# Block-product gates: high weights against paired high and low tokens in one 512-column matmul, weight sums by accumulating transfers

## The chip, the cores and the metric

The kernel runs on one core of one Trainium2 chip. The metric is the device time of one execution in microseconds (us). Three runs of the kernel before took 1444.5, 1445.52 and 1447.1 us, a median of 1445.52 us.

On the core, TensorE (PE) multiplies, VectorE (DVE) and ScalarE (ACT) work on tiles in SBUF and read TensorE's results from PSUM, GpSimd (POOL) does almost nothing in the kernel before, and SyncE (SP) issues every transfer. Each engine executes its own instructions in order and waits on semaphores for the others.

## The reference, cut to what matters

One layer of a hybrid decoder trunk for 512 tokens of 2048 features. From a normalised input `h` come nine projections; two branches (a causal convolution and a differential attention) are gated, projected and merged by sigmoid gates, and projected once more:

```
h = rms_norm(x, g_pre) * (1 + scale) + shift          # shift, scale, gate = split(silu(c) @ w_ada + b_ada)
cv, cg, cz, q, k, v, az, m_conv, m_attn = split(h @ w_in)
y_conv = (silu(layer_norm(conv(cv * sigmoid(cg)))) * silu(cz)) @ w_conv_out
y_attn = (rms_norm(diff_attention(q, k, v)) * (1 - lam0) * silu(az)) @ w_attn_out
out    = (sigmoid(m_conv) * y_conv + sigmoid(m_attn) * y_attn) @ w_o
x      = x + gate * rms_norm(out, g_post)
```

The change concerns three of the projections of `h`: `cz` (1024 columns of `w_in`), `m_attn` and `m_conv` (2048 columns each), called cz, ma and mc in the kernel.

## The kernel before, in words

Features lie on the partitions, tokens along the free axis. Every fp32 operand of a matmul is the sum of two float32r parts, high and low: ACT casts the high part (`split`, L141), DVE subtracts it to get the low part (L142). A product is then three matmuls into one PSUM bank (`mm3`, L163): high by high, high by low, low by high; low by low is left out.

In time the stages are: normalised input and convolution gates (to about 258 us), values, queries, keys and attention (to about 620 us), the az gate with the sums of token blocks (to 679 us), **the gates cz, ma, mc** (679.5 to 1086 us), the projections of the two branches (to 1260 us) and the output projection.

The gates stage is 20 blocks of 256 output columns: four of cz, eight of ma, eight of mc. One block (`gemm_blocks`, L649) cuts `h` into 2x2 blocks (halves of the features by halves of the tokens) and the weights likewise into a11, a12, a21, a22, and computes the result by seven products of block sums instead of eight. The token sums T1 to T4 were made in the stage before (`block_sums`). The weight sums s1 = a21 + a22, s2 = s1 + a11, s3 = a11 + a21 and s4 = s2 + a12 are made in each block by four DVE additions over 128x1024 (L673, L674, L683, L692).

One product multiplies eight 128x128 weight tiles by eight 128x256 token blocks: 8 x 3 matmuls of 256 columns. The seven products use three banks: z (twice), x (three times: T2, T3, T4) and y (twice). In order of time they are z with B11, x with T2, y with T1, x with T3, z with B21, x with T4, y with B22. A later product of a bank adds to what the bank holds, so what DVE needs of the earlier state is read between the two: after x with T2, `u2 = q1 - x` (L679) must have read x before x with T3 may write. q1 is ACT's copy of z (L676). L682, L686, L691 and L695 are the other combinations, one DVE read of 128x256 each.

The raw weights come in two transfers of 1 MB (`wraw`, tiles `wr`, three buffers). The split weights use three buffers each for high (`wh`) and low (`wl`): the split for a product needs the buffer of the product three before it, so it waits for that product to end.

In the ma blocks DVE and ACT also finish the attention output of one head pair, `o * az` (L788), and split it (`oh`, `ol`); o and az are fetched from DRAM by SP, in SP's order behind the spills of the block before.

The matmuls of the stage keep the program's order (a token, `ordered`). The order on DVE and ACT is written out by the Tile framework's scheduler when the kernel is built; nothing in the program fixes it.

Of the kernel before, what the change touches and what calls it, by code (L numbers as in the profile page):

```python
# [51 lines left out]
def hybrid_trunk(ctx: ExitStack, tc: tile.TileContext, x, c, w_ada, b_ada, g_pre, g_post, w_in,  # L52
# [526 lines left out]
    T23, T4 = [None] * KH, [None] * KH  # L579
    t1s = [temp(f"t1_{i}") for i in range(KH // 2)]  # L580

    def block_sums():
        for _ in range(SKIP):
            yield
        for k in range(KH):
# [18 lines left out]
            if k % 2:
                hi, lo = page(f"t4h_{k}", F32R), page(f"t4l_{k}", F32R)
                split(t4, hi, lo, pace=True)
                for i in range(2):
                    T4[k - 1 + i] = (hi[:, i * H2:(i + 1) * H2], lo[:, i * H2:(i + 1) * H2])
                yield
# [17 lines left out]
    B11 = [(hi[:, :H2], lo[:, :H2]) for hi, lo in h[:KH]]  # L627
    T1 = [(hi[:, H2:], lo[:, H2:]) for hi, lo in h[:KH]]
    T2 = [(hi[:, :H2], lo[:, :H2]) for hi, lo in T23]
    T3 = [(hi[:, H2:], lo[:, H2:]) for hi, lo in T23]  # L630
    B21 = [(hi[:, :H2], lo[:, :H2]) for hi, lo in h[KH:]]
    B22 = [(hi[:, H2:], lo[:, H2:]) for hi, lo in h[KH:]]
# [16 lines left out]
    def gemm_blocks(src, c0, name):  # L649
        """Two output tiles [128 features, tokens] of h @ src[:, c0:c0+256], by 7 products of 2x2 blocks.  # L650

        a11 a12 / a21 a22: features by halves of the sum.  Returns (c11 in PSUM, [.. c12], [c21 c22])."""
# [42 lines left out]
        nc.vector.tensor_tensor(u2, u2, y[:, :H2], op=ALU.add)  # L695
        return z, ta, tb

    def silu2(i, z, ta, tb):
# [2 lines left out]
        nc.scalar.activation(g0[:, :H2], z[:, :H2], AF.Tanh, scale=0.5)
        nc.scalar.activation(g0[:, H2:], ta[:, H2:], AF.Tanh, scale=0.5)
        nc.scalar.activation(g1, tb, AF.Tanh, scale=0.5)
        nc.vector.scalar_tensor_tensor(g0[:, :H2], g0[:, :H2], 1.0, z[:, :H2], op0=ALU.add, op1=ALU.mult)
        nc.vector.scalar_tensor_tensor(g0[:, H2:], g0[:, H2:], 1.0, ta[:, H2:], op0=ALU.add, op1=ALU.mult)
        nc.vector.scalar_tensor_tensor(g1, g1, 1.0, tb, op0=ALU.add, op1=ALU.mult)
# [271 lines left out]
```

## Time and profile before

| | us |
|---|---|
| median of 3 runs (lowest, highest) | 1445.52 (1444.5, 1447.1) |
| span of the profiled execution | 1448.4 |
| gates stage in it (first z_cz matmul to first py_ya matmul) | 679.5 to 1085.9 |
| TensorE busy | 1413.6 (98%) |
| VectorE busy | 1053.0 (73%) |
| ScalarE busy | 534.2 (37%) |
| GpSimd busy | 1.8 |

The span runs from the first to the last instruction of the profiled execution; it was 2.9 us longer than the median of the timed runs, so what lies around the span doesn't show as extra time here, and the two differ by less than the spread of the runs (2.6 us) plus 0.3 us. "Busy" counts the engines' own work, not the issuing of transfers. Matmuls overlap in the pipeline, so the mean time of one matmul in the groups (283 ns for 256 columns) is longer than the distance from one matmul to the next; that distance is the length of a run of matmuls in the chain of waits over their count.

### The profile page before, as it was taken

The numbers are of one execution on the slowest core, as the hardware profiler recorded it, in microseconds if no ns is written. First come the engines' busy times: TensorE is split into PE (matmuls) and PEld (weight loads), VectorE is DVE, ScalarE is ACT, GpSimd is POOL, SyncE is SP. The second block draws the span as 40 slices with busy tenths as digits, with TensorE's granted clock in tenths as the row PEclk, the third lists the DMA queues.
The fourth block names the chain that finished last, engine by engine and source line by source line (L and its number), as shares of the span: only waits on it lengthen the run. The fifth ranks groups of instructions, "written<-read, shape, count | busy, mean of one in ns | idle before, by whom it ended". The sixth has DMA issues, their size and how long they took to land.

```text
span 1448.4 us, 20732 instructions
## 1 busy us (share of the span) xinstructions
PE 1413.6 (98%) x8191; PEld 1200.4 (83%) x8191; DVE 1053.0 (73%) x1720; ACT 534.2 (37%) x901; POOL 1.8 (0%) x8
## 2 busy tenths in 40 slices
PE   4999999999999999999999999999999999999997
PEld 4776778787777877688999999999998888888885
DVE  4466785988888888588997888877767448656645
ACT  4622233223444244434544444444445323222230
POOL 0000000000000000000000000000000000000000
PEclk9999999999999999999999999999999999999999
DMA  9878653232223323124654555533369647267543
GB/s 285 264 255 291 215 167 130 88 131 87 66 81 102 102 67 109 66 95 135 209 165 160 187 178 191 188 121 132 126 226 349 224 137 233 95 207 243 189 145 145
DMA packets 178466, 238.62 MB, mean 165 GB/s; under 512 B 7793, under 2 KB 118722, under 8 KB 177474
## 3 DMA queue, kind: packets, MB, share of 16 engines
q1 hardware_dynamic: 178370, 237.31, 49.5%
q8 instruction: 64, 1.05, 0.3%
q14 instruction: 32, 0.26, 0.1%
HBM read 210.02 MB, written 27.26 MB: 164 GB/s over the span
## 4 chain that ended last, share of the span: by engine, by line
PE 93%; DVE 3%; DMA 1%; ACT 1%; issue 1%; SPq 0%; DVEq 0%; ACTq 0%
PE pc L163 12%; PE pw L163 12%; PE py_ya L163 6%; PE py_yc L163 6%; PE pv L163 6%; PE pg_k L163 6%; PE pg_q L163 5%; PE pg_az L163 5%; PE x_ma L163 5%; PE x_mc L163 5%; PE y_mc L163 3%; PE z_mc L163 3%; PE z_ma L163 3%; PE y_ma L163 3%; PE x_cz L163 2%; PE y_cz L163 2%
## 5 line engine op out<-in xcount | busy, mean ns | idle before, releaser
L468 DVE SCALAR_TENSOR_TENSOR cacc<-u,cw,cacc 128x511 f32<-128x511 f32 (+14 forms) x240 | 164.4, 729 | 0.0
L163 PE MATMUL pc<-hh,wh_c 128*128 128x512 f32 x256 | 102.9, 408 | 1.1 <-ACT hh L141 1.1
L163 PE MATMUL pc<-hh,wl_c 128*128 128x512 f32 x256 | 101.0, 398 | 1.5 <-DVE wl_c L142 1.4
L163 PE MATMUL pc<-hl,wh_c 128*128 128x512 f32 x256 | 101.7, 397 | 0.0
L339 DVE TENSOR_TENSOR part<-pc,part 128x512 f32<-128x512 f32 x96 | 66.0, 691 | 46.9 <-PE pc L163 45.8
L163 PE MATMUL pw<-wh_o,mh 128*128 128x512 f32 x224 | 89.0, 397 | 0.0
L163 PE MATMUL pw<-wh_o,ml 128*128 128x512 f32 x224 | 87.3, 390 | 0.0
L163 PE MATMUL pw<-wl_o,mh 128*128 128x512 f32 x224 | 87.2, 389 | 0.0
L141 ACT CAST wh_c<-wr_c 128x1024 fp32r<-128x1024 f32 (+1 forms) x36 | 34.6, 960 | 112.5 <-PE pc L163 85.6
L141 ACT CAST wh_o<-wr_o 128x1024 fp32r<-128x1024 f32 x28 | 29.5, 1053 | 104.5 <-PE pw L163 93.0
L163 PEld LDWEIGHTS pc<-hh,wh_c 128*128 128x128 f32 x256 | 49.0, 192 | 17.9 <-issue 3.3
L856 DVE SCALAR_TENSOR_TENSOR accg<-adag,cact,accg 128x512 f32<-128x512 f32 x60 | 45.0, 750 | 24.0 <-DMA adag<-in_w_ada_dram 22.8
L163 PEld LDWEIGHTS pc<-hh,wl_c 128*128 128x128 f32 x256 | 49.1, 192 | 15.7 <-issue 2.5
L142 DVE TENSOR_TENSOR wl_o<-wr_o,wh_o 128x1024 fp32r<-128x1024 f32 x28 | 34.2, 1221 | 34.0 <-ACT wh_o L141 34.0
L163 PEld LDWEIGHTS pc<-hl,wh_c 128*128 128x128 f32 x256 | 49.3, 192 | 10.2 <-issue 0.4
L163 PE MATMUL pv<-wh_v,hh 128*128 128x512 f32 x128 | 51.2, 400 | 0.9 <-DVE part L339 0.9
L142 DVE TENSOR_TENSOR wl_c<-wr_c,wh_c 128x1024 fp32r<-128x1024 f32 (+1 forms) x36 | 39.7, 1104 | 16.5 <-ACT wh_c L141 16.4
L163 PE MATMUL pg_q<-hh,wh_q 128*128 128x512 f32 x128 | 51.1, 399 | 0.0
L163 PE MATMUL pg_k<-hh,wl_k 128*128 128x512 f32 x128 | 51.1, 399 | 0.0
L163 PE MATMUL pg_q<-hl,wh_q 128*128 128x512 f32 x128 | 50.9, 397 | 0.0
L163 PE MATMUL pg_az<-hl,wh_az 128*128 128x512 f32 x128 | 50.7, 396 | 0.0
L163 PE MATMUL pv<-wl_v,hh 128*128 128x512 f32 x128 | 50.6, 395 | 0.0
(358 smaller groups left out, 4312.7 us busy)
## 6 DMA issues: line engine op xcount, KB each, us to landing
ada<-in_w_ada_dram SPq DMA_DIRECT2D x64, 512.0 KB, 6.1
wr_ma<-in_w_in_dram SPq DMA_DIRECT2D x16, 1024.0 KB, 5.5
wr_mc<-in_w_in_dram SPq DMA_DIRECT2D x16, 1024.0 KB, 5.0
adag<-in_w_ada_dram SPq DMA_DIRECT2D x32, 512.0 KB, 4.2
wr_o<-in_w_o_dram SPq DMA_DIRECT2D x16, 1024.0 KB, 5.1
wr_c<-in_w_in_dram SPq DMA_DIRECT2D x28, 512.0 KB, 5.0
wr_v<-in_w_in_dram SPq DMA_DIRECT2D x8, 1024.0 KB, 5.2
wr_q<-in_w_in_dram SPq DMA_DIRECT2D x8, 1024.0 KB, 5.3
```

The lines of the kernel that those rows point to most:

```text
L141: nc.scalar.copy(hi, src)
L142: i = nc.vector.tensor_tensor(lo, src, hi.bitcast(F32), op=ALU.subtract)
L163: mm = nc.tensor.matmul(ps, a[p], b[q], start=start and i == 0, stop=stop and i == 2, skip_group_check=more)
L339: nc.vector.tensor_tensor(part[i], ps[f], part[i], op=ALU.add)
L468: paced(nc.vector.scalar_tensor_tensor(cvo[t][:, s:], u[t][:, :S - s], wj, cvo[t][:, s:], op0=ALU.mult, op1=ALU.add))
L856: nc.vector.scalar_tensor_tensor(acc, raw[:, k, :], s1, acc, op0=ALU.mult, op1=ALU.add)
```

## The change

- `h` and the token sums are kept in pairs: one tile holds high and low side by side (`pair_of`, `halves_of`), so that [high | low] of 256 tokens each is one 512-column operand. The pages shrink from 59 to 27 beside 16 pairs, the temporaries of the stage from 12 to 10.
- A product is now, for each of the eight weight tiles, one matmul of the high weights by [high | low] over 512 columns into the whole bank, and one of the low weights by high over 256 columns into its first half: 16 matmuls instead of 24.
- A bank thus holds two halves that have to be added. Each combination that was one DVE read becomes two (`comb`, L692; L704, L708 and L709). z is read at its end by an ACT copy and a DVE addition (L718, L719) instead of staying in PSUM for the tanh.
- s1 and s3 are not made on DVE: SP loads a21 a second time into s1 (0.5 MB), and two accumulating GpSimd transfers of 0.5 MB add a22 to s1 and a11 to a21 (which thereby becomes s3) as the data arrives. s2 and s4 stay on DVE (L702, L723).
- Loads are issued one block ahead (`next_load`), and the tanh takes ta and tb whole: two ACT instructions instead of three.

```
-    def gemm_blocks(src, c0, name):
+    def block_load(src, c0, name):
         r1 = wraw(src, 0, KH, c0, 256, f"{name}_1")
         r2 = wraw(src, KH, KH, c0, 256, f"{name}_2")
-        a11, a21 = r1[:, :, :P], r1[:, :, P:]
+        s1 = mp.tile([P, KH, P], F32, tag="s1", bufs=2, name=f"s1_{name}")
+        v = src.rearrange("(t p) n -> p t n", p=P)
+        nc.sync.dma_start(out=s1, in_=v[:, :KH, c0 + P:c0 + 2 * P])
+        nc.gpsimd.dma_start(out=s1, in_=v[:, KH:, c0 + P:c0 + 2 * P], accum_op=ALU.add)
+        nc.gpsimd.dma_start(out=r1[:, :, P:], in_=v[:, :KH, c0:c0 + P], accum_op=ALU.add)
+        blocks[name] = r1, r2, s1
...
         def prod(ps, w, b, first):
             hi, lo = w
+            psv = ps.rearrange("p (a n) -> p a n", a=2)
             for k in range(KH):
-                mm3(ps[:, :H2], (hi[:, k, :], lo[:, k, :]), b[k], first and k == 0, k == KH - 1, not first, ordered)
+                ordered(nc.tensor.matmul(psv, hi[:, k, :], b[k], start=first and k == 0, stop=False,
+                                         skip_group_check=True))
+                ordered(nc.tensor.matmul(ps[:, :H2], lo[:, k, :], b[k][:, 0, :], start=False, stop=k == KH - 1,
+                                         skip_group_check=True))
             pump(rate[0])

+        def comb(out, ps, a, op0, op1):
+            nc.vector.tensor_tensor(out, ps[:, :H2], a, op=op0)
+            nc.vector.tensor_tensor(out, ps[:, H2:], out, op=op1)
...
-        q1, u2 = ta[:, :H2], ta[:, H2:]
+        q1, u2 = tb[:, :H2], ta[:, H2:]
         w11 = wsplit(a11, f"{name}_a11")
-        nc.vector.tensor_tensor(s1, a21, a22, op=ALU.add)
+        prod(z, w11, B11, True)
         nc.vector.tensor_tensor(s2, s1, a11, op=ALU.add)
-        prod(z, w11, B11, True)
         nc.scalar.copy(q1, z[:, :H2])
+        nc.vector.tensor_tensor(q1, z[:, H2:], q1, op=ALU.add)
         ws2 = wsplit(s2, f"{name}_s2")
         prod(xx, ws2, T2, True)
         nc.vector.tensor_tensor(u2, q1, xx[:, :H2], op=ALU.subtract)
+        nc.vector.tensor_tensor(u2, u2, xx[:, H2:], op=ALU.subtract)
         ws1 = wsplit(s1, f"{name}_s1")
         prod(y, ws1, T1, True)
-        nc.vector.tensor_tensor(tb[:, H2:], q1, y[:, :H2], op=ALU.add)
-        nc.vector.tensor_tensor(a21, a11, a21, op=ALU.add)
-        ws3 = wsplit(a21, f"{name}_s3")
+        comb(tb[:, H2:], y, q1, ALU.add, ALU.add)
+        ws3 = wsplit(s3, f"{name}_s3")
         prod(xx, ws3, T3, False)
-        nc.vector.tensor_tensor(tb[:, H2:], xx[:, :H2], tb[:, H2:], op=ALU.subtract)
+        comb(tb[:, H2:], xx, tb[:, H2:], ALU.subtract, ALU.add)
         w12 = wsplit(a12, f"{name}_a12")
         prod(z, w12, B21, False)
+        nc.scalar.copy(ta[:, :H2], z[:, :H2])
+        nc.vector.tensor_tensor(ta[:, :H2], z[:, H2:], ta[:, :H2], op=ALU.add)
         w22 = wsplit(a22, f"{name}_a22")
         prod(xx, w22, T4, False)
...
```

The scheduler writes out another order on DVE for this program. The first two pieces show DVE in a block of ma, between the last combination of the block before and the first ones of this block. In them `wl_ma_s` on `wr_ma_1` is the split of s3, the first `wl_ma_a` on `wr_ma_2` that of a12, the second that of a22; `o` and `ol` are the head's multiplication and split. Before:

```order
L142 TENSOR_TENSOR wl_ma_s_7757<-wr_ma_1_7655,wh_ma_s_7756 128x1024 [waits PE_49,Activation_49]
L142 TENSOR_TENSOR ol_7648<-o_7642,oh_7647 128x512 [waits DMAHW1_49,Activation_49]
L679 TENSOR_TENSOR ta_ma_7664<-ta_ma_7664,x_ma_7660 128x256 [waits DMAHW3_49,PE_49,Activation_49]
L142 TENSOR_TENSOR wl_ma_a_7786<-wr_ma_2_7657,wh_ma_a_7785 128x1024 [waits Activation_49]
L682 TENSOR_TENSOR tb_ma_7665<-ta_ma_7664,y_ma_7661 128x256 [waits PE_49]
L142 TENSOR_TENSOR wl_ma_a_7814<-wr_ma_2_7657,wh_ma_a_7813 128x1024 [waits Activation_49]
```

The read of x (L679) stands ahead of both splits of a12 and a22. The same place of the changed kernel:

```order
L147 TENSOR_TENSOR wl_ma_s_7553<-wr_ma_1_7280,wh_ma_s_7552 128x1024 [waits DMASW3_49,PE_49,Activation_49]
L147 TENSOR_TENSOR wl_ma_a_7575<-wr_ma_2_7282,wh_ma_a_7574 128x1024 [waits PE_49,Activation_49]
L826 TENSOR_TENSOR o_7458<-o_7458,az_7459 128x512 [waits DMAHW7_49,DMAHW6_49,DMAHW3_49]
L147 TENSOR_TENSOR wl_ma_a_7597<-wr_ma_2_7282,wh_ma_a_7596 128x1024 [waits DVE_49,PE_49,Activation_49]
L147 TENSOR_TENSOR ol_7464<-o_7458,oh_7463 128x512 [waits Activation_49]
L704 TENSOR_TENSOR tb_ma_7484<-z_ma_7480,tb_ma_7484 128x256 [waits DMAHW0_49,Activation_49]
L708 TENSOR_TENSOR ta_ma_7483<-tb_ma_7484,x_ma_7481 128x256 [waits DMAHW2_49,DVE_49]
L694 TENSOR_TENSOR tb_ma_7484<-y_ma_7482,tb_ma_7484 128x256
L709 TENSOR_TENSOR ta_ma_7483<-ta_ma_7483,x_ma_7481 128x256 [waits DVE_49]
L695 TENSOR_TENSOR tb_ma_7484<-y_ma_7482,tb_ma_7484 128x256 [waits DVE_49]
```

The two reads of x (L708, L709) now stand behind the splits of a12 and of a22, and behind the head's multiplication, which waits for three transfers. So it is in ma1 to ma7 and, as the last head is finished there, in mc0.

In the blocks mc1 to mc7 no head is in the way, and the order on DVE is this (the split of s3, then that of a12 between the two reads of x):

```order
L704 TENSOR_TENSOR tb_mc_8413<-z_mc_8409,tb_mc_8413 128x256 [waits DMAHW4_49,Activation_49]
L147 TENSOR_TENSOR wl_mc_s_8482<-wr_mc_1_8222,wh_mc_s_8481 128x1024 [waits DMASW5_49,PE_49,Activation_49]
L708 TENSOR_TENSOR ta_mc_8412<-tb_mc_8413,x_mc_8410 128x256 [waits DMAHW6_49,DVE_49,PE_49]
L147 TENSOR_TENSOR wl_mc_a_8504<-wr_mc_2_8224,wh_mc_a_8503 128x1024 [waits Activation_49]
L709 TENSOR_TENSOR ta_mc_8412<-ta_mc_8412,x_mc_8410 128x256 [waits DVE_49]
L694 TENSOR_TENSOR tb_mc_8413<-y_mc_8411,tb_mc_8413 128x256 [waits PE_49]
```

Only the split of a12 stands between L708 and L709 there, and that of a22 comes behind the reads of x and y.

POOL, which had nothing to do in this stage, begins it with these transfers (the last three queue up behind the first):

```order
L668 DMA wr_cz_1_5686<-in_w_in_dram 128x8x128 [waits DMAHW3_49,DMAHW2_49,DMAHW4_49,DMAHW1_49,DMAHW5_49,DMAHW0_49,DMAHW6_49,DVE_49,Activation_49]
L668 DMA wr_cz_1_5694<-in_w_in_dram 128x8x128 [waits DMAHW3_49,DMAHW4_49,DMAHW1_49,DMAHW7_49,DVE_49,Activation_49]
L667 DMA s_cz_5690<-in_w_in_dram 128x8x128 [waits DMAHW3_49,DMAHW2_49,DMAHW6_49,DMAHW0_49,DMAHW7_49,DVE_49,PE_49]
L667 DMA s_cz_5698<-in_w_in_dram 128x8x128 [waits DMAHW3_49]
L667 DMA s_cz_5891<-in_w_in_dram 128x8x128 [waits DMAHW6_49,DMASW2_49,DVE_49]
```

The first s1 (`s_cz`) takes memory that the stage before gives up only at its end, so its load and its accumulation wait for PE and DVE.

## Rows read from the trace of the kernel before

**Rows 1.** The page's busy times: us, share of the span, instructions.
```profile
PE 1413.6 (98%) x8191; PEld 1200.4 (83%) x8191; DVE 1053.0 (73%) x1720; ACT 534.2 (37%) x901; POOL 1.8 (0%) x8
```

**Rows 2.** Busy times by window: us of the window, each engine's busy us, granted clock, DMA.
```profile
core 0: us, PE busy (x) PEld busy (x) DVE busy (x) ACT busy (x) POOL busy (x), PEclk, DMA share, GB/s
800.00:900.00 100.00, 100.00 (x835) 100.00 (x834) 80.46 (x90) 46.88 (x60) 0.00 (x0) 1.00 0.56 184
900.00:1000.00 100.00, 100.00 (x836) 100.00 (x835) 76.92 (x85) 44.43 (x56) 0.00 (x0) 1.00 0.46 151
```

**Rows 3.** Chain of waits, gates: start us, us, instructions.
```profile
982.25 2.88 PE y_mc L163 x24
985.13 2.88 PE z_mc L163 x24
988.01 2.88 PE x_mc L163 x24
```

**Rows 4.** Chain of waits, first branch projection (512-column matmuls).
```profile
1085.93 87.07 PE py_ya L163 x384
```

**Rows 5.** Timeline of ACT around 988 us: start us, us.
```profile
987.98 1.05 ACT L141 CAST wh_mc_s<-wr_mc 128x1024 fp32r<-128x1024 f32 x1 [1.42 <-PE z_mc L163]
988.93 0.37 ACT L676 COPY ta_mc<-z_mc 128x256 f32<-128x256 f32 x1
990.85 1.05 ACT L141 CAST wh_mc_a<-wr_mc 128x1024 fp32r<-128x1024 f32 x1 [1.55 <-issue]
```

**Rows 6.** Timeline of DVE around 990 us.
```profile
989.06 1.23 DVE L142 TENSOR_TENSOR wl_mc_s<-wr_mc,wh_mc_s 128x1024 fp32r<-128x1024 f32 x1 [1.65 <-ACT wh_mc_s L141]
991.00 0.42 DVE L679 TENSOR_TENSOR ta_mc<-ta_mc,x_mc 128x256 f32<-128x256 f32 x1 [0.71 <-PE x_mc L163]
```

**Rows 7.** DVE groups of the gates by shape: count, busy us, mean ns, idle before.
```profile
L142 DVE TENSOR_TENSOR wl_ma_a<-wr_ma,wh_ma_a 128x1024 fp32r<-128x1024 f32 x24 | 29.4, 1223 | 8.1 <-ACT wh_ma_a L141 8.0
L673 DVE TENSOR_TENSOR ws_ma<-wr_ma,wr_ma 128x1024 f32<-128x1024 f32 x8 | 9.8, 1220 | 1.0 <-DMA wr_ma<-in_w_in_dram 1.0
L788 DVE TENSOR_TENSOR o<-o,az 128x512 f32<-128x512 f32 x8 | 5.5, 684 | 0.0
L142 DVE TENSOR_TENSOR ol<-o,oh 128x512 fp32r<-128x512 f32 x8 | 5.5, 683 | 0.0
L679 DVE TENSOR_TENSOR ta_ma<-ta_ma,x_ma 128x256 f32<-128x256 f32 x8 | 3.4, 421 | 1.4 <-PE x_ma L163 0.7
```

**Rows 8.** ACT in the gates: tanh of 128x512.
```profile
983.16 0.63 ACT L781 ACTIVATE mc<-tb_mc 128x512 f32<-128x512 f32 x1
```

**Rows 9.** Transfers issued in the gates: count, KB each, median us to landing.
```profile
wr_ma<-in_w_in_dram SPq DMA_DIRECT2D x16, 1024.0 KB, 5.5
scratch_mc<-mc SPq DMA_DIRECT2D x15, 256.0 KB, 2.0
o<-scratch_o SPq DMA_DIRECT2D x8, 256.0 KB, 5.4
az<-scratch_az SPq DMA_DIRECT2D x8, 256.0 KB, 2.8
```

**Rows 10.** Transfers issued in the first 60 us, same columns.
```profile
ada<-in_w_ada_dram SPq DMA_DIRECT2D x17, 512.0 KB, 8.0
wr_c<-in_w_in_dram SPq DMA_DIRECT2D x2, 512.0 KB, 3.7
```

**Rows 11.** Timeline of PE near 25 us, with the idle time before.
```profile
25.27 1.07 PE L273 MATMUL pa<-ada,c 128*32 128x128 f32 x30 [2.07 <-DMA ada<-in_w_ada_dram]
```

**Rows 12.** Busy times by window, start and end of the program (columns as in rows 2).
```profile
20.00:26.00 6.00, 3.52 (x74) 2.87 (x75) 2.60 (x15) 2.83 (x14) 0.00 (x0) 1.00 1.16 321
26.00:30.00 4.00, 4.00 (x32) 3.79 (x21) 0.29 (x1) 0.80 (x5) 0.00 (x0) 0.57 1.21 294
30.00:34.00 4.00, 2.43 (x36) 1.70 (x36) 2.56 (x7) 3.52 (x9) 0.00 (x0) 0.91 1.11 300
34.00:38.00 4.00, 4.00 (x27) 2.99 (x29) 0.41 (x1) 1.87 (x4) 0.00 (x0) 0.67 0.97 314
38.00:100.00 62.00, 61.95 (x430) 47.54 (x422) 37.46 (x66) 29.85 (x76) 0.00 (x0) 1.00 0.81 268
1440.00:1448.00 8.00, 0.00 (x0) 0.00 (x0) 3.85 (x10) 0.00 (x0) 0.00 (x0) 0.69 0.59 230
```

**Rows 13.** Timeline of PE near 35 us: matmuls of 512 columns.
```profile
33.05 1.92 PE L163 MATMUL pc<-hh,wh_c 128*128 128x512 f32 x4 [1.07 <-ACT hh L141]
34.77 0.63 PE L163 MATMUL pc<-hl,wh_c 128*128 128x512 f32 x1
...
36.48 0.49 PE L163 MATMUL pc<-hl,wh_c 128*128 128x512 f32 x1
...
37.04 0.40 PE L163 MATMUL pc<-hl,wh_c 128*128 128x512 f32 x1
37.27 0.40 PE L163 MATMUL pc<-hh,wl_c 128*128 128x512 f32 x1
```

More of the change, by code (lines that the diff above doesn't have):

```diff
@@ L31 @@
 V_BADA, V_GPRE, V_N0, V_CB, V_CNG, V_CNB, V_SUB, V_N = 0, 32, 48, 48, 56, 64, 72, 73
-NPAGE = 59
+NPAGE = 27
 NTEMP = 14
-NTEMP2 = 12
+NTEMP2 = 10
 PUMP = 5
@@ L204, in hybrid_trunk @@
         nc.vector.memset(halves[64:, 1:2], 1.0)
-        xn = [page(f"xn_{kt}") for kt in range(KT)]
+        xn = []
+        for kt in range(0, KT - 4, 2):
+            g = pair_of(f"xn_{kt}", F32)
+            xn += [g[:, 0, :], g[:, 1, :]]
+        xn += [page(f"xn_{kt}") for kt in range(KT - 4, KT)]
         ss = small(KT, "xss")
@@ L305, in ada @@
                 nc.scalar.activation(hf, xn[k], AF.Identity, scale=scl[:, b:b + 1], bias=sh[:, b:b + 1])
-                hi, lo = page(f"hh_{k}", F32R), page(f"hl_{k}", F32R)
+                hp[k] = pair_of(f"hp_{k}")
+                h[k] = hi, lo = hp[k][:, 0, :], hp[k][:, 1, :]
                 split(hf, hi, lo)
-                h[k] = (hi, lo)
             yield
@@ L578, in hybrid_trunk, with halves_of @@
     KH = KT // 2
-    T23, T4 = [None] * KH, [None] * KH
+    T2, T3, T4 = [None] * KH, [None] * KH, [None] * KH
     t1s = [temp(f"t1_{i}") for i in range(KH // 2)]
+    def halves_of(src, name):
+        g = page(name, F32R)
+        split(src, g[:, :H2], g[:, H2:], pace=True)
+        return g.rearrange("p (a n) -> p a n", a=2)
     def block_sums():
@@ L599, in block_sums @@
             paced(nc.vector.tensor_tensor(t4[:, half], f2[:, :H2], t23[:, :H2], op=ALU.subtract))
-            hi, lo = page(f"t23h_{k}", F32R), page(f"t23l_{k}", F32R)
-            split(t23, hi, lo, pace=True)
-            T23[k] = (hi, lo)
+            T2[k] = halves_of(t23[:, :H2], f"t2_{k}")
+            T3[k] = halves_of(t23[:, H2:], f"t3_{k}")
             yield
[L604 to L609, printed above, removed]
+            T4[k] = halves_of(t4[:, half], f"t4_{k}")
+            yield
     for pair in range(4):
@@ L626, in hybrid_trunk @@
             spill(f"az{hd}", g)
[L627 to L632, printed above, removed]
+    B11 = [g[:, :, :H2] for g in hp[:KH]]
+    T1 = [g[:, :, H2:] for g in hp[:KH]]
+    B21 = [g[:, :, :H2] for g in hp[KH:]]
+    B22 = [g[:, :, H2:] for g in hp[KH:]]
     front.close()
@@ L647, in ordered @@
         tc.stamp_issue_order_token(instruction.ins, "gates")
-    def gemm_blocks(src, c0, name):
+    blocks = {}
+    def block_load(src, c0, name):
         r1 = wraw(src, 0, KH, c0, 256, f"{name}_1")
         r2 = wraw(src, KH, KH, c0, 256, f"{name}_2")
-        a11, a21 = r1[:, :, :P], r1[:, :, P:]
+        s1 = mp.tile([P, KH, P], F32, tag="s1", bufs=2, name=f"s1_{name}")
[4 more added lines that the diff above has]
+        blocks[name] = r1, r2, s1
@@ L694, in gemm_blocks, with silu2 @@
         prod(y, ws4, B22, False)
-        nc.vector.tensor_tensor(u2, u2, y[:, :H2], op=ALU.add)
-        return z, ta, tb
-    def silu2(i, z, ta, tb):
+        comb(u2, y, u2, ALU.add, ALU.add)
+        return ta, tb
+    def silu2(i, ta, tb):
         g0, g1 = temp(f"g0_{i}"), temp(f"g1_{i}")
[L701 to L706, printed above, removed]
+        for g, t in ((g0, ta), (g1, tb)):
+            nc.scalar.activation(g, t, AF.Tanh, scale=0.5)
+            nc.vector.scalar_tensor_tensor(g, g, 1.0, t, op0=ALU.add, op1=ALU.mult)
         return g0, g1
@@ L770, in hybrid_trunk, with next_load @@
     work.append(conv_stats())
+    todo = [(C_CZ + j * 256, f"cz{j}") for j in range(4)]
+    todo += [(c0 + j * 256, f"{name}{j}") for c0, name in ((C_MA, "ma"), (C_MC, "mc")) for j in range(8)]
+    todo = deque(todo)
+    def next_load():
+        if todo:
+            block_load(w_in[0], *todo.popleft())
+    next_load()
     for pair in range(4):
-        gs = silu2(pair, *gemm_blocks(w_in[0], C_CZ + pair * 256, f"cz{pair}"))
+        next_load()
+        gs = silu2(pair, *gemm_blocks(f"cz{pair}"))
         for f in range(2):
@@ L833, in hybrid_trunk @@
     for k in range(8):
-        hi, lo = page(f"yah_{k}", F32R), page(f"yal_{k}", F32R)
+        g = pair_of(f"ya_{k}")
+        hi, lo = g[:, 0, :], g[:, 1, :]
         fetch(f"yah{k}", hi.bitcast(F32))
@@ L867, in hybrid_trunk @@
             k = 2 * j + f
-            g = page(f"mg_{k}")
+            if k % 2 == 0:
+                mgp = pair_of(f"mg_{k}", F32)
+            g = mgp[:, k % 2, :]
             fetch(f"ma{k}", g)
@@ L883, in hybrid_trunk @@
             nc.vector.tensor_tensor(g, mg[k], g, op=ALU.add)
-            hi, lo = page(f"mh_{k}", F32R), page(f"ml_{k}", F32R)
+            m = pair_of(f"mgs_{k}")
+            hi, lo = m[:, 0, :], m[:, 1, :]
             split(g, hi, lo)
```

22 lines of the change are left out of this document (13 added, 9 removed).

## The prediction, made before the run

> **What bounds the kernel now.** I read the busy times first: TensorE works 98% of the span, VectorE 73%, ScalarE 37% and GpSimd nothing [rows 1]. The busy times by window say the same of the gates stage, where the change is: PE is busy 100.00 us of each 100 at granted clock 1.00, with DVE at 77 to 80 [rows 2]. The chain of waits then shows the stage as nothing but products that follow each other, 2.88 us each [rows 3]: 24 matmuls of 256 columns, 0.1200 us apart. So whatever shortens PE's stream counts in full, as long as DVE and ACT feed it in time; and whatever they deliver late counts in full too. There is no idle PE time before that could absorb it.
>
> My sums go against the profiled execution, whose span of 1448.4 us is 2.9 us above the median of the runs, 1445.5. I add the change in time to the median.
>
> **Part 1: the matmuls.** A product keeps its columns (24 x 256 = 8 x (512 + 256)) but has 16 matmuls instead of 24. The projection after the gates shows 384 matmuls of 512 columns in 87.07 us, 0.2267 us each [rows 4]. A new product takes 8 x (0.2267 + 0.1200) = 2.774 us against 2.88: 0.106 us less. There are 20 x 7 = 140: **-14.9 us**, if PE never waits.
>
> **Part 2: work that moves and is hidden.** Per block DVE loses two weight sums of 1.22 us and gains seven reads of 0.42 us [rows 7], so 0.5 us more in some 20, where it now is busy 16. ACT gains a copy of 0.37 [rows 5] and loses a tanh instruction. Both sums that go were behind a PE that never waited, so their removal is worth nothing by itself. In throughput all of this is covered; in order it isn't, which is part 3.
>
> **Part 3: the order on DVE in ma1 to ma7 and mc0.** The x bank is written by the T2 product (second of a block), read by DVE, and written again by the T3 product (fourth). Before, the one read (L679) came 0.28 us after the next product had begun: 991.00 against ACT's 990.85, which itself starts 0.13 us behind it [rows 5, 6]. In the changed order the second read, L709, stands behind the split of a22. The split buffers are three deep, so that split waits for the T1 product (third) to end. T3 can start only after L709, so PE stands from T1's end until the whole row of work is done:
> ACT starts 0.13 after the product's end and casts for 1.05 [rows 5]; DVE follows 0.03 later (989.06 against 987.98 + 1.05) with the split, 1.22 [rows 6, 7]; then `ol`, 0.68, and L704, L708, L694, L709 at 0.42 each, with five gaps of 0.03; then some 0.06 until PE starts. Together 0.13 + 1.05 + 0.03 + 1.22 + 0.68 + 1.68 + 0.15 + 0.06 = 5.0 us.
> The head's multiplication (o by az) stands ahead of that split, and its fetches stand on SP behind the spills of the block before. From the block's start: cast and split of s1 to 2.4, L695 to 2.9, two tanh of 0.63 [rows 8] to 4.2, then the spills and fetches go out. o takes 5.4 us to land [rows 9]: 9.6, and the multiplication 0.68: 10.3. The cast of a22 ends at 3 x 2.774 + 0.13 + 1.05 = 9.5, so the multiplication adds 0.8. **5.8 us in each of 8 blocks, +46.4.** Ends: 5.0 if o and az come as az did, in 2.8 us; 8.4 if they take the 8.0 us of a loaded DMA at the program's start [rows 10]. This kernel moves 1.5 MB more per block.
>
> **Part 4: the other order, mc1 to mc7, and alike cz0, cz3, ma0.** Here only the split of a12 stands before L709. From the block's start: DVE is busy with the last weight sum of the block before (L723) until 0.9, L694 to 1.4, split of s1 to 2.6, L695 to 3.1; ACT two tanh to 4.4, copy of z to 4.8, cast of s3 to 5.8; DVE split to 7.1, L708 to 7.5, split of a12 to 8.8, L709 to 9.2, PE at 9.3. T1 ends at 8.3. 1.0 us each, **+10**, more than the 7 x 0.106 = 0.74 that such a block gains. Ends 0 and 2.0, since the path has some fifteen steps and I know each to about 0.05.
>
> **Part 5: the first block.** The first s1 is placed in memory that is free only when the az stage ends, so its load starts with the first gate product. 512 KB landed in 3.7 us at best and 8.0 at worst [rows 10]. The accumulating transfer isn't in the trace before; GpSimd issues nothing there. The nearest rows bound it: 2.0 us for a 256-KB spill [rows 9], 8.0 for 512 KB in 512-byte runs [rows 10]. I take 3.7, the same size and shape in an unloaded queue. Then 3.7 + 0.3 + 3.7 + 1.22 (s2) + 1.05 (cast) = 10.0 against a product of 2.77: **+7.2**, ends 5.5 and 11.5. Later blocks load one block ahead, and the accumulations have some 20 us for two.
>
> **Part 6: the clock.** At the start PE idled 2.07 us before 25.27 [rows 11] and the granted clock of the next stretch was 0.57, then 0.91, 0.67 and 1.00 [rows 12]. After the pause of 1.07 us at 33.05, eight matmuls of 512 columns came 0.43 us apart, and 0.23 apart from 37.04 [rows 13]: the clock at 1.2 GHz and then at 2.4. That restart cost 8 x 0.2 + 0.1 = 1.7 us. After the last matmuls the clock fell to 0.69 within 8 us [rows 12]. Eight new gaps of 5.8 us and the one of part 5 lie in a stream that otherwise never pauses: **9 x 1.7 = +15.3**. Ends: 0 (the clock stays), 25 (each product behind a gap at half, 2.77 more).
> The page "TensorE: Matmul & The Clock Gate" of the Trainium skill, section "Why this matters for your kernels", says to leave no idle gaps in TensorE between bursts, because the clock falls back to half after one. It speaks against this change, whose gaps are of that kind; by the rule the term is the 15.3, without it 0.
>
> **Sum.** -14.9 + 46.4 + 10 + 7.2 + 15.3 = +64.0; 1445.5 + 64.0 = **1509.5 us**. The ends: all low -14.9 + 40 + 0 + 5.5 + 0 = +30.6 (1476), all high -14.9 + 67 + 20 + 11.5 + 25 = +109 (1554).
>
> **Rivals.**
> 1. *PE's stream sets the time (faster).* DVE is idle 20% of the time and the DMA engines about half [rows 2]; if the reads of x keep ahead of T3, only part 1 is left: 1445.5 - 14.9 = 1430.6. It decides from the point where the stalls are under 0.74 us a block in the mean. Against it stands the printed order: an engine can't read x ahead of a split that stands before it, and that split can't precede T1's end. Chance 0.06.
> 2. *The stalls come, the clock doesn't fall*: parts 1, 3, 4, 5 alone, 1445.5 + 48.7 = 1494, with o and az in time 1488. For it: in the first 100 us the clock is 1.00 over a window with small pauses (61.95 busy of 62.00 [rows 12]). Chance 0.2.
> 3. *The accumulating transfers are the bound.* Two per block must fit into some 20 us, so this decides from 10 us each. At 15 us, blocks take 30 us: 20 x 30 against 406 us, 1640. For it: 512-byte runs took 8.0 us under load [rows 10], and an accumulation may do more per byte. Against it: the DMA share in the stage is about 0.5 [rows 2]. Chance 0.06.
> The page "Collectives: The Full Stack", Part 3, of the Trainium skill states that an add in a transfer needs two source reads and so runs at half the rate of a copy. No row here shows it; by it the accumulation takes 7.4 us instead of 3.7, still under 10, and the sum would be 3.7 us larger through part 5.
> 4. *Larger stalls*: o and az land late with the added traffic (8.4 us in each of 8 blocks, +21), or the clock's term is at its upper end (+10): 1520 to 1550. Chance 0.2.
>
> **How the numbers follow.** The forecast (1495 to 1520) has 0.46, rivals 1 to 4 as above, and 0.02 is left for no change, which would need gain and stalls to cancel. A measurement of this kernel can tell about 0.2%, 2.9 us, from no change. Faster 0.06, same 0.02, slower 0.92. Rival 1 and 3 lie outside the range, with about 0.06 of the tails: 1480 to 1545.
>
> **What would show it.** Right: PE busy in ma windows near 78 of 100, its idle time before x products of T3 ended by DVE (L709), about 6 us each in ma1 to ma7 and mc0, about 1 us in mc1 to mc7; one gap of about 7 us in cz0 behind a GpSimd transfer; granted clock under 1.00 only in the windows with the long gaps; products without a gap at 2.77 us. Wrong: PE busy near 100 in the ma blocks; mc blocks of 19.4 us; PE's idle time ended by GpSimd's transfers throughout; a 512-column matmul into two half banks that isn't 0.227 us behind the next.

## The result, and the profile after

The changed kernel took 1517.03 us (median of 4 runs, 1516.14 to 1518.9) against 1445.78 us of the kernel before (4 runs): 1.0486 times as long, with a 95% interval of 1.0466 to 1.0507, or 71.2 us more. Forecast were 1509.5 us, 64.0 more, with a range of 1480 to 1545.

The page's busy times and slices, which answer to [rows 1]:

```profile
span 1516.9 us, 18768 instructions
...
PE 1422.8 (94%) x7071; PEld 1154.9 (76%) x7071; DVE 1060.9 (70%) x1828; ACT 536.5 (35%) x913; POOL 63.7 (4%) x48
...
PE   5999999999999999988996887889998999999997
...
PEclk9999999999999999998998898999999999999999
DMA  9879633332313222279998778688979875336543
```

TensorE's line of nines now has eights, a seven and a six in slices 18, 19 and 22 to 27, and the granted clock dips in four of these. Waits of PE between 600 and 1200 us say why (columns: us in total, times, longest us; shorter ones are left out):

```profile
PE x_ma L686 <- DVE ta_ma L709: 38.9, 7, 6.1
PE x_cz L686 <- ACT wh_cz_s L146: 9.9, 1, 9.9
PE x_mc L686 <- DVE ta_mc L709: 5.6, 1, 5.6
PE py_ya L168 <- ACT wh_ya L146: 4.0, 1, 4.0
PE x_cz L686 <- DVE ta_cz L709: 1.7, 1, 1.7
...
```

Seven waits in ma1 to ma7 and one in mc0 end at L709, the second read of x, 44.5 us in all; one wait in cz0 is for the first split of a sum; one of 1.7 in cz1 ends at L709 too; one comes after the stage. The windows (columns as in [rows 2]):

```profile
800.00:900.00 100.00, 77.53 (x397) 66.90 (x398) 60.72 (x86) 33.44 (x43) 10.79 (x7) 0.86 0.78 191
900.00:1000.00 100.00, 78.56 (x401) 67.61 (x400) 59.98 (x84) 34.82 (x44) 10.79 (x7) 0.87 0.81 204
...
1050.00:1100.00 50.00, 50.00 (x286) 43.47 (x285) 38.83 (x54) 22.89 (x30) 9.23 (x6) 1.00 0.93 213
...
805.30:810.20 4.90, 4.88 (x16) 4.19 (x17) 0.21 (x1) 0.00 (x0) 0.00 (x0) 0.54 1.03 325
```

PE works 78 of 100 us in ma and all of the time in mc1 to mc7. The last row is the product behind the first long gap: 4.9 us instead of 2.77, at a granted clock of 0.54. And the DMA engines, half idle before, are 0.8 to 0.9 busy.

By stage, profile against profile (before, after): start to the first gate product 679.4 and 673.7; cz 82.4 and 95.7; ma 162.8 and 212.8; mc 161.3 and 165.2; the attention branch's projection 87.1 and 94.1; the rest unchanged. That is -5.7 + 13.3 + 50.0 + 3.9 + 7.0 = 68.5 us between the two spans. The first term can't be put down to the change: it arises in the first 258 us, where the eleven other profiles, taken for the experiments below, differ by some 4 us among themselves (they start the gates at 672.9 to 676.7). Without it the two profiles are 74.2 us apart; the profiled execution of the changed kernel was the slowest of its four runs, 1.9 us above their median.

### The profile page after: what moved, and what is told of

Read it like the earlier page. It is cut to its first block, busy times and chain, and to the rows that moved or that the text cites. A ratio compares the mean times of both kernels' runs of the same rounds, so it can differ in the third digit from the quotient of the medians.

```text
span 1516.9 us, 18768 instructions
## 1 busy us (share of the span) xinstructions
PE 1422.8 (94%) x7071; PEld 1154.9 (76%) x7071; DVE 1060.9 (70%) x1828; ACT 536.5 (35%) x913; POOL 63.7 (4%) x48
## 3 DMA queue, kind: packets, MB, share of 16 engines
q0 software_dynamic: 41600, 20.97, 11.2%
## 4 chain that ended last, share of the span: by engine, by line
PE 84%; DVE 6%; DMA 6%; issue 1%; ACT 1%; SPq 1%; DVEq 0%; ACTq 0%; POOL 0%; POOLq 0%
PE pw L168 12%; PE pc L168 11%; PE py_yc L168 6%; PE pv L168 5%; PE pg_k L168 5%; PE py_ya L168 5%; PE pg_q L168 5%; PE pg_az L168 4%; PE x_ma L686 3%; PE x_mc L686 3%; DMA az<-scratch_az 2%; PE z_ma L686 2%; PE z_mc L686 2%; PE y_mc L686 2%; PE x_mc L688 2%; PE x_ma L688 1%
## 5 line engine op out<-in xcount | busy, mean ns | idle before, releaser
L168 PE MATMUL pc<-hp,wh_c 128*128 128x512 f32 x512 | 162.6, 400 | 0.0
L168 PE MATMUL pw<-wh_o,mgs 128*128 128x512 f32 x448 | 140.6, 393 | 0.0
L168 PEld LDWEIGHTS pc<-hp,wh_c 128*128 128x128 f32 x512 | 95.7, 191 | 27.7 <-issue 5.4
L168 PE MATMUL pc<-hp,wl_c 128*128 128x512 f32 x256 | 100.2, 395 | 1.0 <-DVE wl_c L147 1.0
L168 PEld LDWEIGHTS pw<-wh_o,mgs 128*128 128x128 f32 x448 | 84.1, 188 | 18.9 <-ACT fsq L938 0.7
L168 PE MATMUL pw<-wl_o,mgs 128*128 128x512 f32 x224 | 87.2, 389 | 0.0
L168 PE MATMUL py_ya<-ya,wh_ya 128*128 128x512 f32 x256 | 80.8, 398 | 4.0 <-ACT wh_ya L146 4.0
L168 PE MATMUL pv<-wh_v,hp 128*128 128x512 f32 x256 | 82.9, 397 | 0.9 <-DVE part L348 0.9
L168 PE MATMUL pg_q<-hp,wh_q 128*128 128x512 f32 x256 | 82.7, 398 | 0.0
L168 PE MATMUL pg_az<-hp,wh_az 128*128 128x512 f32 x256 | 81.3, 395 | 0.0
L168 PEld LDWEIGHTS py_ya<-ya,wh_ya 128*128 128x128 f32 x256 | 49.3, 193 | 14.9 <-ACT wh_ya L146 4.5
L168 PEld LDWEIGHTS pc<-hp,wl_c 128*128 128x128 f32 x256 | 48.6, 190 | 12.2 <-DVE wl_c L147 1.5
```

Source lines behind the costliest of these rows:

```text
L168: mm = nc.tensor.matmul(ps, a[p], b[q], start=start and i == 0, stop=stop and i == 2, skip_group_check=more)
```

## The experiments

The kernels are told in their order. Each was timed beside the kernel before on its chip; that one took 1446.9 to 1447.8 us there.

**What holds x's T3 product back.** The chain through the first long gap (start us, us):

```profile
795.71 5.49 DMA az<-scratch_az
...
801.30 0.09 DVE o L826
...
801.91 0.80 DVE wl_ma_a L147
...
803.04 0.69 DVE ol L147
...
804.09 0.42 DVE ta_ma L708
...
804.85 0.34 DVE ta_ma L709
...
805.32 0.77 PE x_ma L686
```

It goes back to the landing of az (801.2), not to T1's end (799.3: that product began at 796.43, and those just ahead of it took 2.83 each). Two waits lie in front of the reads, and e1 to e3 take away one, the other and both.

e1 pins the reads (and only the order on VectorE) ahead of the splits:

```
-        nc.vector.tensor_tensor(u2, q1, xx[:, :H2], op=ALU.subtract)
+        paced(nc.vector.tensor_tensor(u2, q1, xx[:, :H2], op=ALU.subtract))
...
-        w22 = wsplit(a22, f"{name}_a22")
+        w22 = wsplit(a22, f"{name}_a22", pace=True)
```

> The changed kernel, with VectorE's two reads of x (L708, L709) pinned ahead of the splits of a12 and a22; the head's multiplication o*az stays ahead of the reads. Theory (two waits lie side by side, each long enough alone): the split no longer waits for T1's end ahead of the reads, but o*az still starts only about 10.5 us after the block's start, when az has landed; then the cast of oh, ol and four reads (about 3 us in all) follow, so x's T3 product starts some 5 us after T1's end instead of 5.0 to 6.1, and the time falls by 2 to 8 us only, to about 1512. Rival A (the split of a22 is what stalls, as the forecast's term of 5.0 of 5.8 us has it): the gaps shrink to under 1 us and with them the slow products behind them: 8 x (4.8 + 2.1) = 55 less, about 1462. In mc1 to mc7 the small waits of 0.15 us per block go under both.

Measured: 1517.55 us, 1.0476 (1.045 to 1.0503). Waits of PE in ma and mc:

```profile
PE x_ma L686 <- DVE ta_ma L709: 38.4, 7, 6.2
PE x_mc L686 <- DVE ta_mc L709: 5.6, 1, 5.6
```

Rival A fell: with the split out of the way the gaps are the same (5.0 to 6.2 us each), since the head's multiplication still waits for az. The work from its start to the end of L709 is hardly shorter either, 3.6 us instead of 3.9 in the first gap, because `ol` now waits for ACT's cast of `oh` where the split had stood:

```profile
803.21 0.69 DVE L147 TENSOR_TENSOR ol<-o,oh 128x512 fp32r<-128x512 f32 x1 [0.68 <-ACT oh L146]
```

e2 fetches o and az a block earlier; the split stays ahead of the reads:

```
             next_load()
+            if name == "ma":
+                o, az = temp(f"o_{j}"), temp(f"az_{j}")
+                fetch(f"o{j}", o)
+                fetch(f"az{j}", az)
             ta, tb = gemm_blocks(f"{name}{j}")
...
```

> The changed kernel, with o and az of a head fetched one block earlier, so that its multiplication never stands ahead of the reads waiting for a transfer; on VectorE the split of a22 still stands ahead of L708 and L709. Theory (each wait alone is long enough): T1's end + 0.13 + cast 0.95 to 1.05 + split 1.14 + four reads of about 0.35 gives gaps of 4.0 to 4.5 us in ma0 to ma7, 1.5 to 2 in mc0; time 1500 to 1510. Rival B (az's landing alone sets the gap): no gap over 1 us in ma, time about 1456.

Measured: 1507.49 us, 1.0408 (1.0389 to 1.0427).

```profile
PE x_ma L686 <- DVE ta_ma L709: 33.6, 8, 6.4
PE x_mc L686 <- DVE ta_mc L709: 0.9, 1, 0.9
```

Rival B fell too. In ma1 to ma7 the gaps are 3.87 or 3.88 us each: cast, split and four reads behind T1's end, the same in each of these blocks, since no transfer is in it any more. In ma0, which had no gap in the changed kernel, the edit made one of 6.4: there the first head's multiplication now stands ahead of L708 and waits for az, so that e2 also gives back less than it might have.

```profile
782.67 0.69 DVE L827 TENSOR_TENSOR o<-o,az 128x512 f32<-128x512 f32 x1 [2.01 <-DMA az<-scratch_az]
```

e3 takes both away; the multiplication is carried into the next block, behind the split of a22 (`head_end()` after `w22 = wsplit(...)`).

> The changed kernel with both waits taken from in front of the reads: L708 and L709 pinned ahead of the splits of a12 and a22, and the head's multiplication carried over to the next block, behind the split of a22. Theory: no gap over 1 us in ma1 to mc0, so the gaps (44.5 us) and the slow products behind them (8 x 2.1 = 16.8) are gone: 1517 - 61 = 1456, up to 1461 if the multiplication now delays a later read by some 0.5 us per block. Rival C (VectorE's longer work, or the accumulating transfers, hold the ma blocks up by themselves): blocks stay at 22 us or more, time above 1480.

Measured: 1461.22 us, 1.0091 (1.0074 to 1.0108).

```profile
PE x_ma L696 <- DVE tb_ma L705: 2.7, 5, 0.9
...
PE x_mc L696 <- DVE tb_mc L705: 0.5, 1, 0.5
```

The eight gaps are gone, and 56 us with them, at the upper end of what was expected: the read after T3 now comes a little late, 3.2 us in six waits (in e7 below, where the multiplication stands behind that read, they are gone). So the two waits stand side by side: the one for az alone leaves gaps of 5.0 to 6.2 us (e1), the split alone gaps of 3.9 (e2).

**The clock.** e4 fills the gaps with 20 matmuls into a bank that nobody reads:

```
         prod(y, ws1, T1, True)
+        if name[:2] == "ma" and name != "ma0" or name == "mc0":
+            pad = gbank(f"pad_{name}", "o")
+            for i in range(20):
+                ordered(nc.tensor.matmul(pad, hp[0][:, 0, :P], hp[KH][:, :, :H2], start=True, stop=True))
```

> The changed kernel, with 20 more matmuls of 512 columns into a bank that nobody reads between the products T1 and T3 of ma1 to ma7 and mc0: 20 x 0.227 = 4.5 us of work inside gaps of 5.0 to 6.1 us, nothing else changed. Theory (the product behind a gap takes 4.7 to 5.1 us instead of 2.77 because the clock has fallen to half): it takes about 2.8 now, the time falls by 8 x 2.1 = 17 us to about 1500. Rival D (that product is slow because its weights or its reads come late, or for the stall itself): it stays at 4.7 to 5.1 and the time at 1517.

Measured: 1508.93 us, 1.0416 (1.0401 to 1.0432), half of what was expected. The windows of the product behind the first filled gap (1.40 us left of it) and behind the second (2.46 us left):

```profile
804.65:807.50 2.85, 2.85 (x16) 2.51 (x17) 0.19 (x1) 0.00 (x0) 0.00 (x0) 1.00 1.26 277
...
831.35:835.50 4.15, 4.15 (x16) 3.56 (x17) 0.18 (x1) 0.00 (x0) 0.00 (x0) 0.66 0.95 328
```

Where 0.6 to 1.4 us of a gap were left (five of eight), the product behind it took 2.85 us at full clock; where 1.9 to 2.5 us were left, 4.2 to 4.4. Rival D fell: the same instructions behind the same wait are fast when PE was kept busy. The rest of the expected 17 us was not had because three products stayed slow and the gaps together grew from 45.9 to 50.6 us between T1's end and T3.

**The accumulating transfers.** e5 puts them, and the earlier loads, into the kernel before and leaves its matmuls alone (the new `block_load`, without the lines L673 and L683 of before).

> The kernel before (24 matmuls of 256 columns in a product, no half banks) with only the accumulating transfers and the loads one block ahead of the change: s1 and s3 come by GpSimd, VectorE keeps s2 and s4. Theory (the transfers cost only at the start of cz, where s1 finds no memory sooner): one wait before the first x product of cz0 of 7 to 10 us and 2 to 3 us of slow matmuls behind it, no wait over 1 us in ma and mc; time 9 to 13 us above the kernel before. Rival E (the transfers hold the whole stage up, by their own length or by delaying the others): waits in ma and mc, time 25 us or more above before.

Measured: 1460.66 us, 1.0085 (1.0068 to 1.0101).

```profile
PE x_cz L163 <- ACT wh_cz_s L141: 4.0, 1, 4.0
PE x_cz L163 <- DVE tb_cz L692: 3.3, 1, 3.3
PE x_cz L163 <- DVE wl_cz_s L142: 0.8, 1, 0.8
```

The theory holds in size and place: 12.9 us, all of it in cz (96.5 us instead of 82.4); ma and mc took 162.7 and 161.3 us, the same as before. Rival E fell. But it is two waits, not the one of 7 to 10 us: 4.0 in cz0 for the first sum, and 3.3 in cz1, where the read L692 stood behind a subtraction of the convolution's statistics that waited 1.76 us for its fetch: a wait of the same kind as in ma.

e9 makes the accumulations plain loads (`accum_op` left out), so that the sums are not formed.

> The changed kernel with the two GpSimd transfers of a block as plain loads, so nothing is added up (the sums are left out of the computation): same bytes from DRAM, same queue, same instructions on every engine. Theory (an accumulation reads its destination as well, and takes about twice a copy): they land in 4 to 6 us instead of 10.5 to 12.2 (s1) and 6.5 to 7.3 (s3), the wait in cz0 falls from 9.9 to 5 or 6 us, time 1505 to 1512. Rival H (GpSimd's queue itself is slow): landing times and the wait in cz0 stay within 1 us.

Measured: 1519.94 us, 1.0497 (1.0477 to 1.0517). Transfers of the gates stage, first in the changed kernel, then in e9 (columns as in [rows 9]; the line of q0 has packets, MB, share of 16 engines):

```profile
q0 software_dynamic: 40560, 20.45, 35.0%
...
s_ma<-in_w_in_dram POOLq DMA_DIRECT2D x8, 512.0 KB, 10.5
wr_ma<-in_w_in_dram POOLq DMA_DIRECT2D x8, 512.0 KB, 6.5
```

```profile
q0 software_dynamic: 5616, 20.45, 14.4%
...
s_ma<-in_w_in_dram POOLq DMA_DIRECT2D x8, 512.0 KB, 8.3
wr_ma<-in_w_in_dram POOLq DMA_DIRECT2D x8, 512.0 KB, 4.6
```

The expected 1505 to 1512 us were missed. The landing times lie between theory and rival H: a plain load lands 2 us sooner in ma (8.3 and 4.6 us instead of 10.5 and 6.5), and 5.2 and 2.7 us sooner in mc (7.0 and 4.6 instead of 12.2 and 7.3); the wait in cz0 falls from 9.9 to 7.9 us only. The time doesn't fall: the gaps in ma and mc0, which hang on az, come to 44.3 us as against 44.5, and the 2.0 us won in cz0 are lost in cz1 again, where a read stood behind a subtraction that waited for a fetch of the statistics:

```profile
PE x_cz L686 <- DVE tb_cz L695: 2.7, 1, 2.7
```

**Towards a version without the waits.** e7 is e3, with three things more: the sums of cz0 by VectorE, the multiplication `o * az` kept behind the read after T3, and the first two weights of the projection loaded before the last spills.

```
+        if name == "cz0":
+            nc.vector.tensor_tensor(s1, s3, a22, op=ALU.add)
...
+            if name == "mc" and j == 7:
+                for i in range(2):
+                    early_raw[f"ya{i}"] = wraw(w_attn_out[0], 0, 8, i * 256, 256, f"ya{i}")
```

> The changed kernel with all that was found so far put right: reads of x ahead of the splits, the head's multiplication a block later and behind the reads of x's T3 product, the sums of cz0 alone by VectorE as before, and the first two weights of the branch projection loaded before the last block's spills. Theory: of the 71 us lost, the gaps (44.5 + 16.8), the wait in cz0 (9.9 + about 3) and the projection's late weights (4 + 3) go, about 2 us of small waits in cz stay: 1517 - 61 - 13 - 6 = 1437, 1434 to 1444, which is 4 to 12 us under the kernel before. Rival F (what the matmuls save is taken back by late transfers and VectorE elsewhere): 1447 or more.

Measured: 1448.18 us, 1.0002 (0.9992 to 1.0011): rival F, no gain over the kernel before. VectorE in cz0 shows the new wait, ahead of the read that T4 needs:

```profile
690.95 0.69 DVE L784 TENSOR_TENSOR cv<-cv,cmean 128x512 f32<-128x512 f32 x1 [5.47 <-DMA cv<-scratch_cv]
691.55 0.42 DVE L732 TENSOR_TENSOR tb_cz<-x_cz,tb_cz 128x256 f32<-128x256 f32 x1
...
692.49 0.42 DVE L733 TENSOR_TENSOR tb_cz<-x_cz,tb_cz 128x256 f32<-128x256 f32 x1
```

It is the fault of ma once more, with a fetch of the convolution's statistics in the place of az; PE stood 4.25 us, and the product behind took 5.26.

e8 is e7 with all sums on VectorE.

> As e7_ordered, but all weight sums on VectorE as in the kernel before: no accumulating transfer at all, the 512-column matmuls alone. It tells whether the transfers are needed. Theory (VectorE now has 12 reads of 0.35 to 0.42 us instead of 5, and 4 sums of 1.14 to 1.22, some 17.5 us in a block of 19.4): small waits of 1 to 2 us in most blocks, time 1450 to 1470. Rival G (VectorE still fits, and the transfers only cost): 1434 or less, faster than e7_ordered.

Measured: 1452.68 us, 1.0039 (1.0026 to 1.0051). Rival G fell: without the transfers ma takes 169.1 us, with them 160.5.

```profile
PE prs L802 <- DVE rb L801: 5.9, 2, 3.9
```

But the waits in most blocks that the theory expected aren't there. The whole difference lies in one place in ma0: matmuls of the statistics, whose place on PE is fixed, waited 3.9 and 2.0 us for VectorE, and the product behind them took 5.21 us. For the first of the two VectorE had worked without a pause since 752 us; for the second it stood 1.61 us at a sum whose weights hadn't landed. In the rest of ma (780 to 920 us) it is 90% busy against 81% in e7, and keeps up. So the accumulations are worth 4.5 us in this arrangement; whether they still are where the statistics start later, as in e12 below, was not run.

e10 and e11 move the subtraction three and seven products behind its fetch (`for _ in range(3): yield True` after `load("cv", 0)`).

> As e7_ordered, with the first subtraction of the convolution's statistics three products after its fetch instead of one. In e7_ordered VectorE stood 5.47 us for that fetch (cv) in cz0, ahead of the read of x that the T4 product needed: a gap of 4.25 us and a product of 5.26. Theory (what e7_ordered lacks against 1437 is lost in cz): the gap goes, with the slow product 6 to 7 us; cz takes 82 to 85 us instead of 90.6, time 1439 to 1443, below the kernel before by 0.3 to 0.6%. Rival (the fetch waits elsewhere, since the accumulating transfers keep the DMA engines busy): cz stays at 89 or more, time 1446 to 1449.

> As e10_stats_later, with seven products between fetch and subtraction. Same theory: 1438 to 1443; if three products are too few for a fetch of some 6 to 8 us beside the accumulating transfers, this one is faster than e10_stats_later by 3 us or more.

Measured: 1448.63 us, 1.0009 (1.0 to 1.0019), and 1450.69 us, 1.0021 (1.0011 to 1.0031). Both missed their forecast, by the order and not by the reason given. VectorE of e10 in cz0:

```profile
693.84 0.69 DVE L785 TENSOR_TENSOR cv<-cv,cmean 128x512 f32<-128x512 f32 x1 [6.31 <-DMA cv<-scratch_cv]
694.45 0.42 DVE L732 TENSOR_TENSOR tb_cz<-x_cz,tb_cz 128x256 f32<-128x256 f32 x1
```

The scheduler had put the subtraction back where it was; in e11 it stood there too and waited 6.22 us.

e12 starts the statistics after the second block, by their first matmul, whose place on PE is fixed:

```
-    work.append(conv_stats())
...
         gs = silu2(pair, *gemm_blocks(f"cz{pair}"))
+        if pair == 1:
+            work.append(conv_stats())
```

> As e7_ordered, with the convolution's statistics (fetches, subtractions and their matmuls) begun after the second block of cz instead of in the first. In e10 and e11 VectorE's first subtraction had been moved back ahead of the T3 read of cz0 by the scheduler, and waited 6.31 us there (e10) for a fetch that took 10.8 us beside the stage's first loads and accumulations. Theory: with the fetch and its subtraction out of cz0, the gap of 4.2 to 4.6 us and the slow product behind it (1.4 to 2.5) are gone, small waits of 1 to 3 us move to cz2 to ma0; from z_cz to py_ya 398 to 402 us instead of 406.8 (e7) and 408.4 (e10), time 1440 to 1444, under the kernel before. Rival: another wait takes its place there (the weights of cz1, the accumulations), 406 us or more, time 1447 to 1450.

Measured: 1442.47 us, 0.9973 (0.9961 to 0.9985): 0.3% or 4.4 us under the kernel before, a small gain, but the interval leaves out 1. All waits of PE from cz0 to the first projection:

```profile
PE x_cz L699 <- DVE ta_cz L724: 2.0, 1, 2.0
PE x_ma L701 <- DVE wl_ma_s L147: 0.3, 1, 0.3
PE x_cz L701 <- DVE wl_cz_s L147: 0.3, 1, 0.3
PE prs L810 <- DVE rb L809: 0.2, 1, 0.2
```

The gates take 401.7 us there, against 406.4 before.

## Why the prediction was right, step by step

- **Part 1, the matmuls: right in size.** Forecast 2.774 us a product; 69 of the 140 took 2.77 or 2.78. A 512-column matmul into two half banks and its 256-column partner (timeline of PE in mc: start us, us):

```profile
1048.86 0.39 PE L686 MATMUL z_mc<-hp,wh_mc_a 128*128 128x512 f32 x1
1049.09 0.28 PE L688 MATMUL z_mc<-hp,wl_mc_a 128*128 128x256 f32 x1
1049.20 0.39 PE L686 MATMUL z_mc<-hp,wh_mc_a 128*128 128x512 f32 x1
```

  0.23 and 0.11 to 0.12 us apart, as [rows 3, 4] gave it.
- **Part 3, the order on DVE: right.** 5.8 us in each of eight blocks, 46.4 in all, were forecast; measured were 4.96 to 6.10, 44.5 in all, in the eight blocks named. What the sum had wrong is the weight of its two parts: it read the head's multiplication as 0.8 us on top of 5.0. e1 and e2 show two waits that are each long enough alone, the one for az (5.0 to 6.2 us) longer than the split (3.9), so that undoing only the one that was named first gains nothing. And the size is in part luck: in ma1 the multiplication ended 11.2 us after the block's start, where the sum had 10.3, because az landed at 10.4 and not at 9.6; T3 began 3.3 us behind it, where the sum had 3.8.
- **Part 4, mc1 to mc7, cz0, cz3, ma0: wrong.** +10 us were forecast; y and the next x product lost 0.14 + 0.08 us per block in mc (2.92 and 2.85 instead of 2.77), 1.6 us in seven blocks. The step that failed is the sum of some fifteen durations, each with a gap of 0.03 after it. VectorE and ScalarE in mc5:

```profile
1048.55 1.23 DVE L723 TENSOR_TENSOR s_mc<-s_mc,wr_mc 128x1024 f32<-128x1024 f32 x1
1049.69 0.42 DVE L694 TENSOR_TENSOR ta_mc<-y_mc,ta_mc 128x256 f32<-128x256 f32 x1
```

```profile
1051.66 0.63 ACT L818 ACTIVATE mc<-ta_mc 128x512 f32<-128x512 f32 x1 [1.63 <-DVE ta_mc L695]
1052.20 0.62 ACT L819 ACTIVATE mc<-tb_mc 128x512 f32<-128x512 f32 x1
```

  The 1.23-us sum is followed 1.14 us later, the 0.63-us tanh 0.54 us later: instructions that follow each other overlap by 0.09, where the sum had added 0.03. T3 began 8.46 us after the block's start where the sum had 9.3; some seven such pairs make that difference.
- **Part 5, the first block: right place, too small.** +7.2 forecast, 9.9 + 0.5 measured. The load took 4.41 us (3.7 assumed) and the accumulation 8.93 (3.7 assumed, with an upper end of 8.0): the DMA engines were full then (a share of 1.13 from 674 to 677 us). That is 5.9 us more than assumed; the wait grew by only 2.7, because the load went out at 671.02, 2.7 us ahead of the first gate product (673.70) with which the sum had it start, and PE had a matmul of the statistics in between.
- **Part 6, the clock: right in kind, too small.** 1.7 us behind each gap were forecast; the products behind the eight took 4.67 to 5.10 us instead of 2.77, 16.9 us in all, and the one of cz0 some 2.9 more: 19.8 against 15.3. e4 shows that it is the clock. The page "TensorE: Matmul & The Clock Gate" of the Trainium skill (section "Why this matters for your kernels") warns of idle gaps between bursts; the trace agrees, with a granted clock of 0.54 in the window behind such a gap.
- **Rival 3, the transfers as the bound, fell**: two in a block take 10.5 + 6.5 = 17.0 us in ma, whose blocks lasted 26.6, and in e5 and e12 no product of ma or mc waits for them in blocks of some 20 us. The rule weighed beside it ("Collectives: The Full Stack", Part 3, of the Trainium skill) is half the rate for an add, since it needs two source reads; the Trainium skill gives this there for the reduce step of a ring of cores. Here the landing times don't bear out a factor of two: 10.5 against 8.3 us and 6.5 against 4.6 in ma, 12.2 against 7.0 and 7.3 against 4.6 in mc (e9), 1.3 to 1.7 times. The time that the packets took on the DMA engines was 2.4 times as long (35.0% against 14.4%).
- **Rivals 1, 2 and 4.** Rival 1 fell with the 44.5 us of waits in the gates, rival 2 with the slow products behind them (part 6). Of rival 4 the late landing didn't come, no gap being over 6.1 us, while the clock's term did come out above its 15.3, inside its upper end of 25.
- **Not in the sum: the projection behind the gates, +7.0 us.** Its second weight tile was issued on SP only at 1153.15, behind the last block's spills, and PE stood 4.0 us at 1158; the rest is clock (0.50 from 1162.4 to 1167 us). The kernel before had issued it at 1070.95, 15 us before the stage's end. In e7, where it is loaded before the spills, the projection takes 87.1 us again. Part 5 looked at the queue at the start of the stage and nothing looked at its end.

Terms against measured, in us: matmuls -14.9 and -14.8 with 1.9 taken back (below); gaps 46.4 and 44.5; part 4 10 and about 3.5 (mc, and the wait of 1.7 in cz1, where L709 stood behind a subtraction of the statistics that waited 1.37 us for its fetch); first block 7.2 and 10.4; clock 15.3 and 19.8; projection 0 and 7.0. The sum of the second column is 72.3, against 74.2 in the two profiles and 71.2 between the medians. Part 4 was too large and the last three too small, and it is luck that these misses cancelled but for 7 us.

## What to carry to other kernels

When a change adds reads between two uses of a bank, the printed order on the reading engine tells more than its busy share: look for every instruction ahead of the read, ask for each what it waits for, and count on having to remove all of them, since two waits that are each long enough hide each other. An engine order that a scheduler writes has to be pinned by something that it can't move, such as a matmul of fixed place. Of a chain of many short instructions add the distances from start to start, not the durations.

## What the runs showed that was not expected

- At full granted clock the products have two lengths, 2.77 and 2.83 us. In the changed kernel 34 of 140 took 2.80 to 2.83, in e12 nearly all of mc, in e7 hardly any there. In e12, where some 90 products took the longer time, that is 5 of the 14.9 us that the matmuls save. Nothing here tells what sets it; it stays open.
- An accumulating transfer of the same bytes goes in smaller packets than the plain load: 40560 against 5616 packets for 20.45 MB (e9), some 500 bytes each against 3600, and 35.0% against 14.4% of the DMA engines. Beside them the 1-MB weight loads of ma took 8.2 us to land, 6.9 beside plain loads (e9), and 5.5 in the kernel before [rows 9].
- The profiled execution of before reached the gates 2.7 to 6.5 us later than the other profiles. The difference is there by the first matmul of the values (258.3 us; 252.4 in the changed kernel, and 255.6 in e5, which has the code of before in that stage); the cause stays open.
